# First pair's queries made inside the projection's last block, and the v blocks put ahead of the c blocks

## The chip, the core and the metric

The kernel runs on one core of a Trainium2 chip. The metric is the device time of one execution in microseconds (us). The engines are named as in the profile: PE (TensorE matmul), DVE (VectorE), ACT (ScalarE), POOL (GpSimd), and SP, which here only issues DMAs.

## The reference

Two layers of a hybrid block run over 1024 latent tokens and 256 context tokens, with a model width of 1024. Each layer computes:

```
h = modulated RMSNorm of x (latent) and ctx (context)
q, k, v, z_a, b, a, q_a, kv_a, z_b, hh, bg, cg, z_c = split(h @ w_in)
A: q,k,v = silu(depthwise conv of q,k,v); gated DeltaNet over chunks of 64 rows, both directions, 4 heads of 128
B: queries = rmsnorm(q_a) @ w_qb, rotary on 32 of 96 columns; keys, values = rmsnorm(kv_a) @ w_kvb;
   softmax attention of 4 heads, times silu(z_b)
C: bg * conv3(cg * hh) * silu(z_c)
x = x + gate * (concat(A, B, C) @ w_out)
```

The context goes through the same layer in layer 0. In layer 1 it feeds only keys, values and the DeltaNet state. All is in float32.

## The kernel before

**Precision.** Every wide product is made of three fp32r products: a tensor is split into a high part (a copy by ACT, L75) and a low part (a subtraction, L76, on DVE for the weights), and high x high, high x low and low x high are summed in PSUM. In the trace `h_hi`, `h_lo` and `w` are such parts; `h_c` are those of the 256 context tokens.

**The projection.** `run_blocks(blocks, hooks)` (L766) walks over 24 blocks of 128 output columns. A block is a weight load of 512 KB (`load`), its split into a buffer pair of pool W8 (`split`), and 24 matmuls for each group of tokens (512, 512, and the context's 256; layer 1 leaves the context out for the q, z and c blocks). While block q runs on PE, block q+2 is split and block q+3 is loaded; W8 has two buffers. The list `bl` holds in this order: four k blocks; q and z_a blocks mixed, six; eight c blocks (two groups of four: pad, times gate, convolution of three taps, times gate, times silu); four v blocks; two z_b blocks. A v or k or q block is followed by a convolution of five taps (L458 to L498): its taps are `L466`, one DVE instruction each, four of them on DVE. After a v block there come transposes on PE (L516), a scaling on DVE (`L519`, tile `sg`) and a store of `sg` to the scratch `vr_d` (L530). A z_b block ends in a silu by ACT (L566, tile `zs`) and a store to `zb_d` (L568). `sg`, `zs`, the padded rows and the accumulators share pool T5, which has five buffers.

**Beside it.** `hooks` start other work at given blocks: the preparation of the DeltaNet chunks, the inverse of their 32-row bases (L669 to L685, a chain of 31 steps of `L680` and `L681` on DVE in each of three batches), the merges of the inverses into `N` and `nn_d` (L700 to L760), and at block 21 the lanes `kv_lane`. A lane loads 128 token rows of the key and value part (`mk`, L824), transposes them on PE (L827, L828) and copies the parts into `ckv` (128 rows) and `pes` (rotary rows).

**The queries.** `load_qkv` runs behind the split of the last block but one: it loads the query and key weights, scales and splits them into `wq` (pool W8) and `wk`, and starts `q_rows`, which loads the query rows (`mq`) and a rotary table (`rot`), transposes them (L854, L855) and splits them into `qa` and `qb`. `q_head` makes one head's queries: five matmuls (L84, `qa,wq` and `qb,wq`), then an ACT copy, two rotary products on DVE (L883, L884), their sum on POOL (L885), an ACT copy (L79, `qt<-r`), and two subtractions for the low part (L887 on POOL, L888 on DVE). `mk`, `mq`, `rot`, `qb`, `r1`, `r2` and `wk_r` share pool P2, which has seven buffers.

**The attention's opening.** From L1280 on PE's instructions stand in written order; the other engines' order is made by a scheduler in all of the program. The opening calls `key_rope` (the rotary rows `pes` are copied by DMA into `kh`, `kl` and, for the context, `kc`; L1060), then `q_head` for the first pair of heads, then `k_pair` (the pair's keys: L84, `ckv,wk`), then the scores of the attention (L1104, transposed, `kh,qt` and `kc,qt`) are mixed with the DeltaNet scan, whose operands come by DMA into `ring` tiles from `vr_d`, `nn_d`, `kt_d` and `qk_d` (L1203, L1206). The first scan product is L1238. All DMAs of the program are issued by SP, in order, on one queue.

Of the kernel before, what the change touches and what calls it, by code (L numbers as in the profile page):

```python
# [8 lines left out]
F32R = mybir.dt.float32r  # L9
ACTF = mybir.ActivationFunctionType  # L10
ALU = mybir.AluOpType
# [17 lines left out]
def kernel(  # L29
# [27 lines left out]
    def st(shape, tag, dtype=F32, name=None):  # L57
        return sb.tile(shape, dtype, tag=tag, name=name or tag, bufs=BUFS[tag])
# [10 lines left out]
    V, A, P, T, S = nc.vector, nc.scalar, nc.gpsimd, nc.tensor, nc.sync  # L69
# [4 lines left out]
    def split(raw, hi, lo, eng=V):  # L74
        A.activation(out=hi, in_=raw, func=ACTF.Copy)  # L75
        eng.tensor_tensor(out=lo, in0=raw, in1=hi.bitcast(F32), op=ALU.subtract)  # L76

    def copy_a(out, in_):
        A.activation(out=out, in_=in_, func=ACTF.Copy)  # L79
# [41 lines left out]
    sch = Sched()  # L121
# [194 lines left out]
    for l in range(DEPTH):  # L316
        last = l == DEPTH - 1
        n_act = NX if last else NT
        col = LY[l]["col"]
# [113 lines left out]
        def parts(n_tok):  # L433
            return [(g, t0, n, 2 + t0 if g < 2 else 1030) for g, (t0, n) in enumerate(GROUPS) if t0 < n_tok]
# [331 lines left out]
        def run_blocks(blocks, hooks):  # L766
            n = len(blocks)
            for q in range(n):
                if q in hooks:
                    hooks[q]()  # L770
                b = blocks[q]
                for n_g, (g, _, w, _) in enumerate(parts(b.n_tok)):
                    b.mm(g)
                    if n_g == 0 and q > 1 and blocks[q - 2].post1:
                        blocks[q - 2].post1(blocks[q - 2])
                if q + 2 < n:
                    blocks[q + 2].split()
                if q + 3 < n:
                    blocks[q + 3].load()
                if q == n - 2:  # L780
                    load_qkv()
                b.post0(b)


        qkv = {}
        sc = 96.0 ** -0.5

        def load_qkv():
            wq_r = st([128, 2, 4, 128], "P4", name="wq_r")
            hq = mla_w_qb[l].rearrange("p (h f) -> p h f", h=4)  # L790
            S.dma_start(out=wq_r[:, 0, :, 0:96], in_=hq[0:128])
            for r in range(2):
                S.dma_start(out=wq_r[64 * r:64 * r + 64, 1, :, 0:96], in_=hq[128:192])
            wk_r = st([128, 512], "P2", name="wk_r")
            for w in range(2):
                S.dma_start(out=wk_r[:, 256 * w:256 * w + 256].rearrange("p (h f) -> p h f", h=4),
                            in_=mla_w_kvb[l].rearrange("p (h s f) -> s p h f", h=4, s=2)[w])
            wq = st([128, 4, 4, 128], "W8", F32R, name="wq")
            for b_ in range(2):
                V.tensor_scalar(wq_r[:, b_, :, 0:96], wq_r[:, b_, :, 0:96], col[:, 75 + b_:76 + b_], sc, ALU.mult, ALU.mult)  # L800
                P.tensor_scalar(wq_r[:, b_, :, 96:128:2], wq_r[:, b_, :, 65:96:2], -1.0, None, ALU.mult)
                P.tensor_copy(out=wq_r[:, b_, :, 97:128:2], in_=wq_r[:, b_, :, 64:96:2])
            split(wq_r[:, 0], wq[:, 0], wq[:, 1])
            copy_a(wq[:, 2], wq_r[:, 1])
            V.tensor_tensor(out=wq[0:64, 3], in0=wq_r[0:64, 1], in1=wq[0:64, 2].bitcast(F32), op=ALU.subtract)
            P.memset(wq[64:128, 3].bitcast(F32), 0.0)
            wk = st([128, 2, 512], "P4", F32R, name="wk")
            V.tensor_scalar(wk_r, wk_r, col[:, 77:78], None, ALU.mult)
            split(wk_r, wk[:, 0], wk[:, 1])
            qkv.update(wq=wq, wk=wk)  # L810
            sch.add(q_rows(qgs[0]))

        kvf = Flags()

# [22 lines left out]
        qgs = [g for g in (0, 1, 2) if g < 2 or not last]  # L837
        QA, Q = {}, {}
# [54 lines left out]
        bl = [conv_block("k", h) for h in range(4)]  # L893
        bl += [conv_block("q", 0), z_block(O_ZA, 2, za_d), conv_block("q", 1), z_block(O_ZA, 3, za_d)]
        bl += [conv_block("q", h) for h in range(2, 4)]
        bl += [c_block(j, q) for j in range(2) for q in range(4)]
        bl += [conv_block("v", h) for h in range(4)]
        bl += [z_block(O_ZB, j, zb_d) for j in range(2)]
        todo = [0, 1, 2, 3, 8, 9, 4, 5, 6, 7] if last else list(range(NT))

# [21 lines left out]
        if l == 0:  # L922
# [16 lines left out]
            for t in (0, 1):  # L939
                for hf in range(2):  # L940
                    pms = [bank(), bank()]
                    for k4 in range(2):
                        for j in range(2):
                            q = 2 * hf + j
# [91 lines left out]
        if last:  # L1036
            sch.add(adas())
        run_blocks(bl, {4: start_prep, 5: start_base, 11: start_prep_q, 8: start_merge, 21: start_kv})
        sch.until(lambda: len(kvf) == NT)
        wk, ckv, pes = qkv["wk"], qkv["c"], qkv["pe"]  # L1040
# [151 lines left out]
        units = []  # L1192
# [91 lines left out]
        def heads(u):  # L1284
            return [(u["g"], 2 * u["pair"] + r) for r in range(2)]

        key_rope()
        sch.until(lambda: qgs[0] in QA)
        for gh in heads(units[0]):
            q_head(*gh)  # L1290
        for _ in k_pair(0):
            pass
        sch.tick(3.0)
# [257 lines left out]
```

## Time and profile before

| | us |
|---|---|
| median of 3 runs (1711.97, 1713.01, 3195.78) | 1713.01 |
| the profiled execution | 1712.38 |
| its span, first to last instruction | 1710.7 |
| PE busy (96% of the span) | 1648.7 |
| DVE busy (64%) | 1095.8 |
| ACT busy (44%) | 760.1 |
| POOL busy (37%) | 632.7 |

The mean granted clock of TensorE is 0.984 of full speed. An engine's busy time is the time in which at least one of its instructions ran. In the rows below, `x8` behind a tile's name is a count of instructions, and a square bracket gives the idle time of the engine just before the instruction and what ended it. The projection of layer 0 ends on PE at 545 us, that of layer 1 at 1366 us; the opening of the attention follows each.

### The profile page before, as it was taken

How to read it: one execution, taken by the hardware profiler on the slowest of the kernel's cores; microseconds unless marked ns; L12 is line 12 of the kernel's file. 1: busy time of each engine (PE TensorE's matmuls, PEld its weight loads, DVE VectorE, ACT ScalarE, POOL GpSimd, SP SyncE). 2: the span in 40 equal slices, each digit the busy share in tenths (PEclk: the TensorE clock that was granted, in tenths of full speed). 3: DMA queues.
4: the chain of work that ended last, by engine and by line, in shares of the span. 5: the costliest groups of instructions: out<-in, count | busy, mean ns of one | idle time of the engine just before them, and what ended most of it. 6: DMA issues, size and time to landing. Idle time of an engine off the chain costs nothing.

```text
span 1710.7 us, 29900 instructions
## 1 busy us (share of the span) xinstructions
PE 1648.7 (96%) x10964; PEld 1311.5 (77%) x10964; DVE 1095.8 (64%) x2041; ACT 760.1 (44%) x1909; POOL 632.7 (37%) x848
## 2 busy tenths in 40 slices
PE   7999999999998999998999999999999979999998
PEld 5887888787887877765788887777777768776586
DVE  2534648888355767765566345589996577766664
ACT  4744554422444543344354435544335444434432
POOL 0420334332221456557331211544222135557731
PEclk9999999999999899999999999999999989999999
DMA  9332466464145745544442313564543464555541
GB/s 359 129 127 79 156 210 226 126 206 163 59 133 144 253 160 180 184 145 148 145 142 98 120 56 114 180 206 159 191 133 110 128 214 163 161 185 161 175 157 49
DMA packets 195402, 266.54 MB, mean 156 GB/s; under 512 B 50528, under 2 KB 115248, under 8 KB 195256
## 3 DMA queue, kind: packets, MB, share of 16 engines
q1 hardware_dynamic: 195256, 264.64, 47.5%
q8 instruction: 87, 1.43, 0.3%
q14 instruction: 59, 0.48, 0.1%
HBM read 182.71 MB, written 79.17 MB: 153 GB/s over the span
## 4 chain that ended last, share of the span: by engine, by line
PE 71%; DVE 10%; DMA 7%; issue 4%; ACT 3%; POOL 3%; SPq 1%; DVEq 0%; POOLq 0%; ACTq 0%
PE bank L452 27%; PE bank L84 23%; PE bank L1161 4%; PE bank L1238 2%; PE bank L1257 2%; PE bank L1104 2%; PE bank L1251 2%; PE bank L1256 2%; DVE pr L680 2%; PE bank L1228 2%; DVE Mb L681 1%; PE bank L516 1%; DVE acc L466 1%; POOL gcb L617 1%; DMA wa<-in_w_ada_dram 1%
## 5 line engine op out<-in xcount | busy, mean ns | idle before, releaser
L452 PE MATMUL bank<-h_hi,w 128*128 128x512 f32 x1664 | 432.4, 402 | 2.4 <-DVE h_hi L283 2.4
L452 PEld LDWEIGHTS bank<-h_hi,w 128*128 128x128 f32 x1664 | 303.6, 188 | 74.6 <-issue 4.5
L452 PE MATMUL bank<-h_lo,w 128*128 128x512 f32 x832 | 216.5, 401 | 0.0
L452 PEld LDWEIGHTS bank<-h_lo,w 128*128 128x128 f32 x832 | 153.3, 188 | 37.3 <-issue 2.1
L466 DVE SCALAR_TENSOR_TENSOR acc<-pad,col,acc 128x1284 f32<-128x1284 f32 (+1 forms) x104 | 157.4, 1513 | 10.5 <-ACT acc L463 8.3
L1131 POOL TENSOR_TENSOR vt<-vt,probT 128x512 f32<-128x512 f32 x110 | 143.7, 1324 | 19.0 <-ACT probT L1145 18.1
L84 PE MATMUL bank<-wo_hi,mix 128*128 128x512 f32 x576 | 146.7, 405 | 1.6 <-ACT wo_hi L75 1.3
L1145 ACT ACTIVATE probT<-bank 128x512 f32<-128x512 f32 (+1 forms) x168 | 96.5, 590 | 98.7 <-PE bank L84 92.3
L84 PEld LDWEIGHTS bank<-wo_hi,mix 128*128 128x128 f32 x576 | 109.3, 192 | 29.0 <-ACT wo_hi L75 2.8
L76 DVE TENSOR_TENSOR w<-wr,w 128x1024 fp32r<-128x1024 f32 x52 | 65.4, 1260 | 97.5 <-ACT w L75 97.4
L1106 DVE TENSOR_REDUCE mx<-bank 128x1 f32<-128x512 f32 (+1 forms) x200 | 108.5, 584 | 10.1 <-PE bank L1104 8.9
L452 PE MATMUL bank<-h_c,w 128*128 128x256 f32 x816 | 109.1, 286 | 0.0
L452 PEld LDWEIGHTS bank<-h_c,w 128*128 128x128 f32 x816 | 101.5, 188 | 6.1 <-issue 4.1
L75 ACT ACTIVATE w<-wr 128x1024 fp32r<-128x1024 f32 x52 | 55.0, 1061 | 85.0 <-PE bank L452 66.1
L84 PE MATMUL bank<-qt,kh 97*128 97x512 f32 (+1 forms) x256 | 84.5, 411 | 3.6 <-ACT probT L1145 3.3
L1161 PE MATMUL bank<-probT,vt 128*64 128x512 f32 (+1 forms) x336 | 81.1, 605 | 0.0
L1234 POOL TENSOR_TENSOR ring<-ring,qx 128x512 f32<-128x512 f32 x32 | 41.5, 1298 | 93.4 <-DMA ring<-row_d 71.2
L681 DVE TENSOR_TENSOR Mb<-Mb,pr 128x31 f32<-128x31 f32 (+15 forms) x186 | 70.4, 379 | 5.0
L84 PE MATMUL bank<-wo_lo,mix 128*128 128x512 f32 x288 | 73.5, 395 | 0.0
L680 DVE TENSOR_TENSOR pr<-L,Mb 128x31 f32<-128x31 f32 (+15 forms) x186 | 69.7, 375 | 4.8
L617 POOL TENSOR_TENSOR gcb<-gcb,gc 128x1024 f32<-128x1024 f32 x20 | 43.6, 2184 | 67.4 <-DMA gcb<-row_d 43.0
L522 ACT ACTIVATE jk<-bank 128x128 f32<-128x128 f32 x152 | 42.1, 277 | 51.5 <-PE bank L516 29.2
(309 smaller groups left out, 3201.4 us busy)
## 6 DMA issues: line engine op xcount, KB each, us to landing
wr<-in_w_blk_dram SPq DMA_DIRECT2D x52, 512.0 KB
wa<-in_w_ada_dram SPq DMA_DIRECT2D x32, 512.0 KB
gcb<-row_d SPq DMA_DIRECT2D x20, 512.0 KB
nn_d<-N SPq DMA_DIRECT2D x20, 512.0 KB
ring<-vr_d SPq DMA_DIRECT2D x40, 256.0 KB
ring<-nn_d SPq DMA_DIRECT2D x40, 256.0 KB
qk_d<-gcb SPq DMA_DIRECT2D x18, 512.0 KB
ring<-kt_d SPq DMA_DIRECT2D x36, 256.0 KB
```

Source lines behind the costliest of these rows:

```text
L75: A.activation(out=hi, in_=raw, func=ACTF.Copy)
L76: eng.tensor_tensor(out=lo, in0=raw, in1=hi.bitcast(F32), op=ALU.subtract)
L84: T.matmul(outp, lhsT=lh, rhs=rh, start=q == 0, stop=q == n - 1)
L452: T.matmul(pb[:, 0:n], lhsT=self.w[:, wi, k, :], rhs=hg[g][hi][:, k, :], start=q + k == 0, stop=q == 2 and k == KD - 1)
L466: V.scalar_tensor_tensor(out=acc[:, 2:hi], in0=pad[:, 2 + t - r:hi + t - r], scalar=col[:, ci:ci + 1], in1=acc[:, 2:hi], op0=ALU.mult, op1 ...
L617: P.tensor_tensor(gcb, gcb, bc(gc[:, i, :], 128), ALU.subtract)
L680: V.tensor_tensor(out=pv, in0=bc(L[:, 0:k, k], w), in1=N[:, k:k + 1, k:32].to_broadcast([128, k, w]), op=ALU.mult)
L681: V.tensor_tensor(out=N[:, 0:k, k:32], in0=N[:, 0:k, k:32], in1=pv, op=ALU.subtract)
L1106: V.tensor_reduce(mx[:, gk:gk + 1], pb[:, 0:n], AX.X, ALU.max)
L1131: P.tensor_tensor(acc, a0, a1, ALU.add)
L1145: A.activation(out=pts[r][:, kk, 0:n], in_=pb, func=ACTF.Exp)
L1161: T.matmul(u["po"][64 * r:64 * r + 64, 0:n], lhsT=vx[:, kt, hh * 64:hh * 64 + 64], rhs=pts[r][:, kk, 0:n], start=kt == keys[0], stop=kt == ...
```

## The change

The list of blocks has the four v blocks ahead of the eight c blocks. `load_qkv` is cut in two: loads, scaling and the split of the key weights run one block earlier (at `n - 3`), and the new `split_qkv`, at the old place, splits the query weights and starts `first_queries`, which is `q_rows` followed by `q_head` for the first pair's two heads. The opening of the attention no longer calls `q_head`; it waits, in the building of the program, for both heads to have been placed. Lines from the middle on stand 12 further down (L1104 is L1116, L824 is L836, L885 is L897, L1060 is L1072).

```diff
--- before.py
+++ after.py
@@ -777,8 +777,10 @@
                     blocks[q + 2].split()
                 if q + 3 < n:
                     blocks[q + 3].load()
+                if q == n - 3:
+                    load_qkv()
                 if q == n - 2:
-                    load_qkv()
+                    split_qkv()
                 b.post0(b)
 
 
@@ -795,20 +797,30 @@
             for w in range(2):
                 S.dma_start(out=wk_r[:, 256 * w:256 * w + 256].rearrange("p (h f) -> p h f", h=4),
                             in_=mla_w_kvb[l].rearrange("p (h s f) -> s p h f", h=4, s=2)[w])
-            wq = st([128, 4, 4, 128], "W8", F32R, name="wq")
             for b_ in range(2):
                 V.tensor_scalar(wq_r[:, b_, :, 0:96], wq_r[:, b_, :, 0:96], col[:, 75 + b_:76 + b_], sc, ALU.mult, ALU.mult)
                 P.tensor_scalar(wq_r[:, b_, :, 96:128:2], wq_r[:, b_, :, 65:96:2], -1.0, None, ALU.mult)
                 P.tensor_copy(out=wq_r[:, b_, :, 97:128:2], in_=wq_r[:, b_, :, 64:96:2])
+            wk = st([128, 2, 512], "P4", F32R, name="wk")
+            V.tensor_scalar(wk_r, wk_r, col[:, 77:78], None, ALU.mult)
+            split(wk_r, wk[:, 0], wk[:, 1])
+            qkv.update(wq_r=wq_r, wk=wk)
+
+        def first_queries():
+            yield from q_rows(qgs[0])
+            for h in range(2):
+                yield 1.2
+                q_head(qgs[0], h)
+
+        def split_qkv():
+            wq_r = qkv["wq_r"]
+            wq = st([128, 4, 4, 128], "W8", F32R, name="wq")
             split(wq_r[:, 0], wq[:, 0], wq[:, 1])
             copy_a(wq[:, 2], wq_r[:, 1])
             V.tensor_tensor(out=wq[0:64, 3], in0=wq_r[0:64, 1], in1=wq[0:64, 2].bitcast(F32), op=ALU.subtract)
             P.memset(wq[64:128, 3].bitcast(F32), 0.0)
-            wk = st([128, 2, 512], "P4", F32R, name="wk")
-            V.tensor_scalar(wk_r, wk_r, col[:, 77:78], None, ALU.mult)
-            split(wk_r, wk[:, 0], wk[:, 1])
-            qkv.update(wq=wq, wk=wk)
-            sch.add(q_rows(qgs[0]))
+            qkv["wq"] = wq
+            sch.add(first_queries())
 
         kvf = Flags()
 
@@ -893,8 +905,8 @@
         bl = [conv_block("k", h) for h in range(4)]
         bl += [conv_block("q", 0), z_block(O_ZA, 2, za_d), conv_block("q", 1), z_block(O_ZA, 3, za_d)]
         bl += [conv_block("q", h) for h in range(2, 4)]
+        bl += [conv_block("v", h) for h in range(4)]
         bl += [c_block(j, q) for j in range(2) for q in range(4)]
-        bl += [conv_block("v", h) for h in range(4)]
         bl += [z_block(O_ZB, j, zb_d) for j in range(2)]
         todo = [0, 1, 2, 3, 8, 9, 4, 5, 6, 7] if last else list(range(NT))
 
@@ -1285,9 +1297,7 @@
             return [(u["g"], 2 * u["pair"] + r) for r in range(2)]
 
         key_rope()
-        sch.until(lambda: qgs[0] in QA)
-        for gh in heads(units[0]):
-            q_head(*gh)
+        sch.until(lambda: (qgs[0], 1) in Q)
         for _ in k_pair(0):
             pass
         sch.tick(3.0)
```

The first place is SP's queue at the end of layer 0's projection. `mk` are the key rows of the last lanes, `kh`, `kl` and `kc` take the rotary rows, `ring` are the scan's operands, `zb_d` is the store of the last z_b block. Before:

```order
L824 DMA mk<-mla_d 128x160 x4
L530 DMA vr_d<-sg 128x10x128
L1060 DMA kh<-pes 33x2x1024
L1060 DMA kl<-pes 32x2x1024
L1060 DMA kh<-pes 33x2x1024
L1060 DMA kl<-pes 32x2x1024
L1203 DMA ring_5671<-vr_d 128x512
L1203 DMA ring_5671<-nn_d 128x512
L1060 DMA kc<-pes 33x2x256
L568 DMA zb_d<-zs 128x1280
L1060 DMA kc<-pes 32x2x256
```

And now:

```order
L836 DMA mk<-mla_d 128x160 x3
L1072 DMA kh<-pes 33x2x1024 x2
L1072 DMA kl<-pes 32x2x1024
L836 DMA mk<-mla_d 128x160
L1072 DMA kl<-pes 32x2x1024
L1215 DMA ring_5703<-vr_d 128x512
L1215 DMA ring_5703<-nn_d 128x512
L1215 DMA ring_5703<-kt_d 128x512
L1218 DMA ring_5703<-qk_d 128x512
L568 DMA zb_d<-zs 128x1280
L1072 DMA kc<-pes 33x2x256
```

The store `vr_d` has gone from this place, the last lane's `mk` stands behind three copies out of `pes`, and the first `kc` stands behind two more `ring` loads and the `zb_d` store.

The second place is the same stretch of SP's queue in layer 1. Before:

```order
L568 DMA zb_d<-zs 128x1024
L760 DMA nn_d<-N 128x1024
L824 DMA mk<-mla_d 128x160 x4
L530 DMA vr_d<-sg 128x10x128
L824 DMA mk<-mla_d 128x160 x2
L568 DMA zb_d<-zs 128x1024
L1060 DMA kh<-pes 33x2x1024
```

And now:

```order
L568 DMA zb_d<-zs 128x1024
L760 DMA nn_d<-N 128x1024
L836 DMA mk<-mla_d 128x160 x3
L568 DMA zb_d<-zs 128x1024
L836 DMA mk<-mla_d 128x160 x4
L1072 DMA kh<-pes 33x2x1024 x2
L1072 DMA kl<-pes 32x2x1024
```

The `mk` loads of the last four lanes now stand behind the store of the last z_b block instead of ahead of it. Of these four loads the built program lets the first wait for POOL's L897 of the first head and the third for POOL's L899 of that head, whose tiles `r2` and `r1` had their buffers of P2, and the fourth for the transposes of the first.

The third place is DVE in layer 0's projection, among the steps of the base inverse; here a piece of the difference, with - for before and + for now:

```order
 L681 TENSOR_TENSOR Mb<-Mb,pr 128x28x4
 L680 TENSOR_TENSOR pr<-L,Mb 128x135
+L466 SCALAR_TENSOR_TENSOR acc<-pad,col_103,acc 128x1284
 L681 TENSOR_TENSOR Mb<-Mb,pr 128x27x5
+L466 SCALAR_TENSOR_TENSOR acc<-pad,col_103,acc 128x1284
 L680 TENSOR_TENSOR pr<-L,Mb 128x156
+L708 STREAM_TRANSPOSE tt<-tt 128x256
+L216 TENSOR_TENSOR A_105<-bank,col_107 128x2x2
+L466 SCALAR_TENSOR_TENSOR acc<-pad,col_103,acc 128x1284
 L681 TENSOR_TENSOR Mb<-Mb,pr 128x26x6
```

The taps of the v blocks' convolutions now stand between the steps of the inverse, where the c blocks' products stood.

On PE, the ten matmuls of the first pair's queries stand in layer 0 ahead of the last block's 24 context matmuls (`h_c,w`), where they stood behind them, and in layer 1 among the last block's eight last `h_hi,w` matmuls. In layer 1 the transposes of the last seven lanes stand behind that block, where four lanes' stood.

## Rows read from the trace of the kernel before

**Rows 1.** Page, chain that ended last: shares of the span by engine.

```profile
PE 71%; DVE 10%; DMA 7%; issue 4%; ACT 3%; POOL 3%; SPq 1%; DVEq 0%; POOLq 0%; ACTq 0%
```

**Rows 2.** Windows, both projections: length, busy us PE, PEld, DVE, ACT, POOL, clock, DMA share, GB/s.

```profile
300.00:420.00 120.00, 118.56 (x1040) 95.51 (x1040) 102.79 (x214) 36.33 (x104) 37.34 (x51) 1.00 0.49 158
420.00:540.00 120.00, 120.00 (x1236) 97.52 (x1235) 58.04 (x83) 52.64 (x120) 24.16 (x53) 1.00 0.35 110
1160.00:1280.00 120.00, 120.00 (x1040) 95.97 (x1039) 111.07 (x232) 42.71 (x117) 42.27 (x67) 1.00 0.53 171
1280.00:1360.00 80.00, 79.50 (x931) 63.78 (x931) 47.45 (x62) 42.39 (x94) 16.94 (x39) 1.00 0.37 117
```

**Rows 3.** Timeline, SP, layer 0: start, duration, queue and line, [idle before <- releaser].

```profile
546.90 1.27 SPq L1203 DMA_DIRECT2D ring<-nn_d  x1
548.28 0.88 SPq L1060 DMA_DIRECT2D kc<-pes  x1
549.21 0.50 SPq L568 DMA_DIRECT2D zb_d<-zs  x1
549.81 3.24 SPq L1060 DMA_DIRECT2D kc<-pes  x3
```

**Rows 4.** Timeline, PE, layer 0, opening of the attention.

```profile
545.11 0.87 PE L84 MATMUL bank<-qa,wq 128*128 128x512 f32 x3
...
547.46 1.91 PE L84 MATMUL bank<-ckv,wk 128*128 128x512 f32 x9
...
550.65 0.50 PE L1104 MATMUL bank<-kh,qt 96*128 96x512 f32 x1 [1.29 <-ACT qt L79]
...
554.99 0.55 PE L1104 MATMUL bank<-kc,qt 96*128 96x256 f32 x1 [3.26 <-DMA kc<-pes]
```

**Rows 5.** Chain in order of time, layer 0: start, duration, what.

```profile
548.28 6.57 DMA kc<-pes
```

**Rows 6.** Windows, layer 0, two microseconds at the wait for `kc`.

```profile
552.00:554.00 2.00, 0.00 (x0) 0.00 (x0) 2.00 (x5) 1.92 (x4) 1.93 (x3) 0.75 0.89 324
```

**Rows 7.** Timeline, PE, layer 1, opening of the attention.

```profile
1366.93 0.30 PE L827 MATMUL bank<-cst,mk 128*128 128x128 f32 x1 [0.77 <-DMA mk<-mla_d]
...
1367.31 0.94 PE L84 MATMUL bank<-qa,wq 128*128 128x512 f32 x3
...
1374.19 0.51 PE L1104 MATMUL bank<-kh,qt 96*128 96x512 f32 x1 [2.58 <-ACT qt L79]
...
1377.37 0.79 PE L1104 MATMUL bank<-kh,qt 96*128 96x512 f32 x1 [1.97 <-ACT qt L79]
...
1383.43 2.05 PE L1238 MATMUL bank<-ring 128*128 128x128 f32 x8 [1.25 <-DMA ring<-nn_d]
...
1402.56 0.27 PE L1115 MATMUL bank<-cst,nm 128*8 128x128 f32 x1 [2.17 <-DVE nm L1109]
```

**Rows 8.** Timeline, SP, layer 1.

```profile
1363.45 1.55 SPq L824 DMA_DIRECT2D mk<-mla_d  x2
...
1368.81 0.94 SPq L1060 DMA_DIRECT2D kh<-pes  x1
...
1376.06 0.67 SPq L1203 DMA_DIRECT2D ring<-vr_d  x1
```

**Rows 9.** Chain in order of time, layer 1.

```profile
1362.68 3.84 DMA vr_d<-sg
...
1366.61 1.09 ACT zs L566 x2
```

**Rows 10.** Lines 466 and 519: ns min/median/max, first and last start, forms.

```profile
L466 DVE SCALAR_TENSOR_TENSOR acc<-pad,col,acc x104: 1164/1555/1925, 138.2 to 1343.8; 128x1284 f32<-128x1284 f32 x84, 128x1024 f32<-128x1024 f32 x20
...
L519 DVE TENSOR_TENSOR sg<-bank,rki x24: 411/680/693, 480.5 to 1362.2; 128x512 f32<-128x512 f32 x16, 128x256 f32<-128x256 f32 x8
```

**Rows 11.** Lines 884 and 885, the queries' rotary products and their sum.

```profile
L884 DVE TENSOR_TENSOR r<-bank,rot x16: 695/696/697, 547.8 to 1525.0; 32x512 f32<-32x512 f32 x16
...
L885 POOL TENSOR_TENSOR r<-r,r x16: 1255/1266/1280, 548.7 to 1525.8; 32x512 f32<-32x512 f32 x16
```

## The prediction

> **What bounds the kernel now.** I read the chain that ended last first: 71% of the span is PE, 10% DVE and 7% DMA [rows 1]. So a change pays where PE stands idle, or costs where it makes PE wait. Then I read windows of the two projections. PE is full there, and the resource with least room is DVE: from 300 to 420 us it is busy for 102.79 of 120 us and from 1160 to 1280 us for 111.07 of 120, while the stretches behind them leave it half free (58.04 of 120, 47.45 of 80) [rows 2]. PE was still busy for 118.56 and 120.00 us in the tight stretches, so what DVE owes is covered by the lead of the weight splits, about one block.
>
> Last come the two openings of the attention, in PE's timeline. In layer 0 the query matmuls start at 545.11 us, `k_pair` at 547.46, and then PE waits twice: 1.29 us for `qt` from ACT and 3.26 us for `kc` from a DMA [rows 4]. The DMA wait is the harder of the two: the chain runs from the first `kc` issue through 6.57 us of transfer [rows 5], and that issue follows right behind the ring loads [rows 3]. In layer 1 PE waits 2.58 us and 1.97 us, both for `qt`, then 1.25 us for a ring load, and later 2.17 us for DVE [rows 7]. These waits are the whole stake: 1.29 + 2.58 + 1.97 = 5.84 us is what the queries' chain visibly costs.
>
> **Part 1, the queries inside the last block.** The ten matmuls are moved, not removed: from 545.11 to 547.46 us they took 2.35 us [rows 4], and they take as much inside the block, so PE's busy time is unchanged. What leaves the opening is the chain behind them: ACT copy, two DVE products of 0.695 us, a POOL sum of 1.266 us, ACT again [rows 11]. All of the 5.84 us goes if nothing else is late at the same instant. So I ask what is.
>
> *Layer 0.* The score that waited 1.29 us is followed by the one that waits for `kc`, so an earlier `qt` only lengthens the second wait. What counts is when `kc` lands. The last lane's `mk` now stands behind three copies out of `pes`, which wait for the lanes before; these stand among the query matmuls, which have moved ahead of the context matmuls, so I put the first copy near 543.7 us, an estimate from that place. By the issue times of such copies (0.88 us, three in 3.24 us [rows 3]) `mk` is issued some 3 us later, at 546.7, and needs about 3 us to be used (in layer 1 two loads are issued from 1363.45 for 1.55 us, and the transposes start at 1366.93 [rows 7, 8]); with its copies on ACT and DVE the context's rotary rows are there near 550.5, so the first `kc` goes at 550 to 551 instead of 548.28. With the same 6.57 us it lands 1.7 to 2.7 us later. It also stands behind `kt`, `qk` and `zb_d` now, 256 + 256 + 640 KB by their shapes. At the 324 GB/s that the queue moved in this stretch [rows 6] these are 3.6 us if they must all pass first, and nothing if they overlap. I take +2.5 us, near the end of unchanged landing, since the ring loads ahead of `kc` before [rows 3] are already in the 6.57 us; the bounds are 0 (copies no later than now) and +6.
>
> The Trainium skill, page "DMA: Bandwidth & Descriptors", section "Queues, rings and completion order", says that SP owns one ring on each engine and that descriptors are consumed in ring order there. By that rule the 3.6 us count in full, and layer 0 would cost +5 to +6 rather than +2.5; the landing of 6.57 us for 66 KB behind larger loads agrees with it, though it doesn't separate queueing from the issue of the three further copies.
>
> *Layer 1.* Before, the last two `mk` loads wait behind the store `vr_d` and go at 1363.45 [rows 8]; their transposes start at 1366.93 [rows 7]. Now the last four stand behind the second `zb_d`, which needs the silu of the last block. The query matmuls lengthen that block by some 2.4 us, three lanes' transposes leave it (about 0.7 us), so it ends near 1367.4 and its silu (1.09 us for two [rows 9], one is left) near 1368. Then the first load's buffer must be released by POOL's sum: the first head's matmuls end near 1366, plus the ACT copy, 2 x 0.69 on DVE and 1.27 on POOL [rows 11] is about 1369. The third load waits for one more ACT copy and POOL subtraction, 1371; the fourth for the transposes of the first, 1369 + 2.9 + 0.3 = 1372.2, and lands near 1375.5. The first rotary copy `kh` then goes at about 1376 instead of 1368.81; eight such copies took until 1376.06, when the ring loads begin [rows 8]. So the ring loads start up to 6.6 us later, and the scan product at 1383.43 [rows 7], which was waiting for one, moves with them; the vanished waits of 2.58 and 1.97 are swallowed on the way. Something comes back: 4 x 0.69 us of the queries' DVE work is out of the opening, which shortens the DVE wait of 2.17 us at 1402.56. Also, the store `vr_d` with its 3.84 us, for which the last silu waited [rows 9], is gone from this place, so the block's end may come earlier than I have it. I take +5 us; the bounds are -4.5 (both `qt` waits gone, nothing later) and +8.
>
> **Part 2, v ahead of c.** Neither the work nor PE's count of matmuls changes; DVE's is shifted. A v block costs four taps of 1.555 us and a scaling of 0.68 + 0.68 + 0.41 (1.77): 8.0 us, four of them 32 us. A group of four c blocks costs two taps and three products of the shape of that scaling: 3.1 + 5.3 = 8.4 us [rows 10]. So the tight stretch, in which one such group stood, gets about 23 us more of DVE work in each layer. Its free DVE time was 120 - 102.79 = 17.2 us in layer 0 and 8.9 us in layer 1 [rows 2]; 6 to 14 us overflow into the freer stretch behind. The cover is the lead of the splits, about one block (a block with three groups takes near 15 us of PE, one with two groups near 12). I put the stalls at +1 us in all, from 0 to +4 while the cover holds; if it is gone the overflow itself is the price, 6 + 14 = 20 us. The loads and scaling that `load_qkv` does one block earlier lie in a stretch where DVE and POOL are half idle, as the second and fourth of the rows show [rows 2]: 0. The two stores `cx_d` that now take the place of `vr_d` near the end have no reader at the opening: 0.
>
> **The sum.** +2.5 + 5 + 1 = +8.5 us on the profiled execution's 1712.4, so 1721 us. The median of the runs, 1713.0, is 0.6 us above the profiled one, which I leave out.
>
> **Rivals.**
>
> *The waits simply go* (chance 0.22). If the lanes' loads are not late, the seams lose 1.29 + 2.58 + 1.97 = 5.8 us, and up to 8 with the DVE wait of 2.17 [rows 7]: 1704 to 1707. For it speaks that `vr_d` leaves the queue in front of the lanes' loads; against it the loads' new place behind `zb_d` and the POOL releases.
>
> *It cancels* (chance 0.22). Layer 0 stays bound by `kc` as it was, layer 1 loses its `qt` waits and gains as much for `ring`: 1709 to 1716.
>
> *DVE becomes the bound of the projection: slower* (chance 0.12). In the tight stretch a weight split is queued behind a v block's four taps and the inverse's steps, and PE waits for `w`. It decides when the overflow exceeds the lead of about 12 to 15 us; layer 1's 14 us is right at it. The price is up to 20 us, with the seams as forecast 1712.4 + 20 + 7.5 = 1740. Against it: the trace shows PE full with DVE at 93% [rows 2], and inverse steps may yield to splits.
>
> In a sentence of its own: the Trainium skill, "GPSIMD Engine Reference", states that VectorE and GpSimd share their SBUF interfaces, which would make those DVE operations longer than their medians; `L466`, with a median of 1555 ns, reaches 1925 [rows 10], which would agree, and it would only raise the price of this rival.
>
> The forecast has 0.44. My range goes from the best of the first rival, 1704, to 1736, which takes in the upper bounds of both seams (1712.4 + 6 + 8 + 4 = 1730) and part of the DVE case.
>
> **Chances by size.** 2% (34 us) is about what a measurement of this kernel tells from no change: faster means under 1679, slower over 1747. No case reaches the first, and only the worst of the DVE case the second: 0.02, 0.94, 0.04.
>
> **What would show it.** In the changed profile, layer 0: `kc` issued after 550 us relative to a projection that ends at 545, and PE's wait before the first `kc` score over 4 us. Layer 1: no `qt` wait, but a gap before `k_pair` or the first score that ends on `mk`, `pes` or `kh`, `mk` loads issued singly behind `zb_d`, and ring loads some 6 us later against the end of the last block. Projections: PE busy 118 to 120 in each 120 us; a gap before `L452` that ends on DVE `w` would favour the DVE case. If the lanes' last transposes lie within 2 us of the last block's end, my layer 1 term is wrong and the first rival holds.

## The result

The changed kernel takes 1729.13 us (median of six runs, 1720.80 to 1733.78), the kernel before 1711.95 us. The ratio is 1.0101, with a 95% interval from 1.0083 to 1.0119: about 17 us slower, a change of less than 2%. One of the six runs before took 3195.78 us, the others 1707.54 to 1713.01. The profiled execution is the fastest of the six, 1720.8 us with a span of 1719.0, so the trace below shows half of the loss (8.3 us of span); a second trace of the same kernel, taken in the experiments, shows more of it.

To see where the time went I set marks in both traces: a first and the last projection matmul of each layer (L452; the count begins in layer 0 with the first matmul of the context's tokens, `h_c,w`, at 104 us, and in layer 1 with its first projection matmul, near 930 us), and the first update of the scan's state behind the opening (`bank<-vd,ring`). All in us:

| | layer 0 projection | from its end to the first state update | layer 1 projection | from its end to the first state update | span |
|---|---|---|---|---|---|
| before | 440.9 | 19.3 | 435.0 | 23.6 | 1710.7 |
| changed | 444.1 | 16.2 | 444.7 | 24.8 | 1719.0 |
| changed, second trace | 446.4 | 16.7 | 449.8 | 26.3 | 1733.9 |

The ten query matmuls, 2.35 us, have moved from the openings into the projections, and the transposes of one lane in layer 0 and of three in layer 1 (0.22 us each) the other way, so +2.1 and +1.7 us of the projections are no loss. Layer 0 as a whole comes out even in the first trace (+3.2 and -3.1). Layer 1's projection is where the time is: +9.7 us in the first trace and +14.8 of the second trace's +23.2. In it PE stands idle for 8.3 us before, for 13.5 us in the first trace and 18.4 in the second. The four windows of [rows 2], in the profile of the changed kernel:

```profile
300.00:420.00 120.00, 116.17 (x1036) 95.00 (x1035) 108.58 (x190) 46.38 (x112) 39.12 (x60) 1.00 0.54 167
420.00:540.00 120.00, 120.00 (x1234) 97.06 (x1233) 49.41 (x106) 43.53 (x112) 21.54 (x44) 1.00 0.33 105
1160.00:1280.00 120.00, 114.64 (x968) 94.39 (x967) 115.28 (x203) 46.20 (x108) 41.07 (x66) 0.99 0.53 166
1280.00:1360.00 80.00, 79.35 (x939) 60.51 (x939) 40.21 (x85) 33.12 (x85) 17.80 (x38) 1.00 0.37 113
```

PE was busy for 118.56 and 120.00 us of the tight stretches; now it is for 116.17 and 114.64. DVE has gone from 102.79 to 108.58 and from 111.07 to 115.28, and it has become lighter behind them. PE's timeline shows the longest new waits there, two in each layer:

```profile
353.66 0.45 PE L720 MATMUL bank<-tt,Mm 32*32 32x32 f32 x32 [1.68 <-DVE tt L709]
...
385.14 0.45 PE L720 MATMUL bank<-tt,Mm 32*32 32x32 f32 x32 [2.15 <-DVE tt L709]
...
1203.87 3.39 PE L452 MATMUL bank<-h_hi,w 128*128 128x512 f32 x8 [2.50 <-DVE tt L738]
...
1232.27 0.23 PE L729 MATMUL bank<-tt 32*32 32x32 f32 x4 [1.91 <-ACT tt L723]
```

None of them waits for a weight. L720 and L729 are steps of the merges, which stand at fixed places in PE's order; L720 needs a scaling on DVE (L709), L729 a copy by ACT (L723). The third wait is that of a projection matmul that the profile puts behind L738, a merge's scaling that reads from a PSUM bank. The eight matmuls behind the third wait took 3.39 us (why is told at the end).

The openings, in the order of [rows 3], [rows 4], [rows 7] and [rows 8]. Layer 0, SP and then PE:

```profile
547.37 1.57 SPq L836 DMA_DIRECT2D mk<-mla_d  x1
...
552.06 0.37 SPq L568 DMA_DIRECT2D zb_d<-zs  x1
...
554.20 3.21 SPq L1072 DMA_DIRECT2D kc<-pes  x4
```

```profile
552.91 0.45 PE L839 MATMUL bank<-cst,mk 128*128 128x128 f32 x1 [4.44 <-DMA mk<-mla_d]
...
553.23 3.55 PE L84 MATMUL bank<-ckv,wk 128*128 128x512 f32 x9
...
558.60 0.35 PE L1116 MATMUL bank<-kc,qt 96*128 96x256 f32 x1 [0.33 <-DMA kc<-pes]
...
560.44 2.21 PE L1250 MATMUL bank<-ring 128*128 128x128 f32 x16
```

The last lane's `mk` went at 547.37 and the first `kc` at 554.20 instead of 548.28, behind `zb_d`. Against the end of the projection that is 5.7 us instead of 3.0; the forecast, 550 to 551 with an end at 545.3, was 4.7 to 5.7. PE waits 4.44 us for `mk` where it waited 1.29 for `qt`, but the 3.26 us for `kc` have shrunk to 0.33, and 16 scan products run without the 0.85 us wait for DVE that split them before. All waits of PE from the projection's end to the first state update add up to 5.0 us against 5.4. Layer 1, SP and PE:

```profile
1375.05 0.32 SPq L568 DMA_DIRECT2D zb_d<-zs  x1
...
1375.78 3.54 SPq L836 DMA_DIRECT2D mk<-mla_d  x4
...
1380.17 1.87 SPq L1072 DMA_DIRECT2D kh<-pes  x2
...
1387.42 0.59 SPq L1215 DMA_DIRECT2D ring<-vr_d  x1
```

```profile
1378.30 0.45 PE L839 MATMUL bank<-cst,mk 128*128 128x128 f32 x1 [3.03 <-DMA mk<-mla_d]
...
1381.23 3.34 PE L84 MATMUL bank<-ckv,wk 128*128 128x512 f32 x9
...
1388.39 0.55 PE L1116 MATMUL bank<-kc,qt 96*128 96x256 f32 x1 [3.00 <-DMA kc<-pes]
...
1391.93 4.15 PE L1250 MATMUL bank<-ring 128*128 128x128 f32 x16 [1.28 <-DMA ring<-nn_d]
```

The four `mk` stand behind the store at 1375.05, take 3.54 us to issue, the rotary copies start 6.0 us after the end of the projection (3.1 before), and the ring loads 13.3 us after it (10.3 before). The waits for `qt` are gone; waits for `mk`, `kc` and a ring load have their place, 8.3 us in all against 7.3. Behind the waits for `mk` the granted clock is 0.50 (from 552 to 558 us and from 1378 to 1384 us), and `k_pair`'s nine matmuls take 3.55 and 3.34 us instead of 1.91 and 1.90.

### The profile page after: what moved, and what is told of

Same layout as the page of the kernel before. It is cut to its first block, busy times and chain, and to the rows that moved or that the text cites. A ratio compares the mean times of both kernels' runs of the same rounds, so it can differ in the third digit from the quotient of the medians.

```text
span 1719.0 us, 29914 instructions
## 1 busy us (share of the span) xinstructions
PE 1646.0 (96%) x10964; PEld 1309.0 (76%) x10964; DVE 1095.4 (64%) x2041; ACT 759.3 (44%) x1909; POOL 632.7 (37%) x848
## 4 chain that ended last, share of the span: by engine, by line
PE 74%; DVE 9%; DMA 6%; issue 4%; POOL 3%; ACT 3%; SPq 1%; POOLq 0%; DVEq 0%; ACTq 0%
PE bank L452 30%; PE bank L84 22%; PE bank L1173 3%; PE bank L1250 2%; PE bank L1269 2%; PE bank L1263 2%; PE bank L1268 2%; PE bank L1116 2%; PE bank L1240 2%; DVE acc L466 1%; DVE Mb L681 1%; PE bank L188 1%; DVE pr L680 1%; DMA wa<-in_w_ada_dram 1%; PE bank L516 1%
## 5 line engine op out<-in xcount | busy, mean ns | idle before, releaser
L452 PE MATMUL bank<-h_hi,w 128*128 128x512 f32 x1664 | 434.9, 403 | 4.9 <-DVE tt L738 2.5
L452 PEld LDWEIGHTS bank<-h_hi,w 128*128 128x128 f32 x1664 | 305.1, 189 | 77.9 <-issue 7.2
L452 PE MATMUL bank<-h_lo,w 128*128 128x512 f32 x832 | 215.7, 400 | 0.0
L452 PEld LDWEIGHTS bank<-h_lo,w 128*128 128x128 f32 x832 | 153.4, 188 | 37.4 <-issue 2.1
L452 PE MATMUL bank<-h_c,w 128*128 128x256 f32 x816 | 108.2, 286 | 0.1
L452 PEld LDWEIGHTS bank<-h_c,w 128*128 128x128 f32 x816 | 101.6, 189 | 6.2 <-issue 4.1
L84 PEld LDWEIGHTS bank<-wo_lo,mix 128*128 128x128 f32 x288 | 54.1, 188 | 13.1
```

Of the source, the lines that this page charges most:

```text
L84: T.matmul(outp, lhsT=lh, rhs=rh, start=q == 0, stop=q == n - 1)
L452: T.matmul(pb[:, 0:n], lhsT=self.w[:, wi, k, :], rhs=hg[g][hi][:, k, :], start=q + k == 0, stop=q == 2 and k == KD - 1)
```

## The experiments

The marks of all of them, one traced execution each (the ratios are of several runs, each against the kernel before run beside it):

| | ratio to before, 95% interval | layer 0 projection | opening | layer 1 projection | opening |
|---|---|---|---|---|---|
| before | 1 | 440.9 | 19.3 | 435.0 | 23.6 |
| order alone | 1.0097 (1.0078 to 1.0115) | 444.5 | 16.0 | 448.3 | 24.4 |
| queries alone | 1.0030 (1.0010 to 1.0050) | 442.3 | 17.1 | 437.8 | 22.3 |
| changed, again | 1.0120 (1.0101 to 1.0139) | 446.4 | 16.7 | 449.8 | 26.3 |
| two taps left out | 1.0052 (1.0033 to 1.0071) | 440.3 | 16.5 | 443.7 | 25.7 |
| v between the c groups | 1.0145 (1.0127 to 1.0163) | 450.1 | 16.1 | 452.8 | 22.9 |
| paired key rows | 1.0119 (1.0099 to 1.0140) | 445.3 | 16.6 | 449.6 | 27.2 |
| queries alone, paired | 1.0024 (1.0010 to 1.0038) | 443.5 | 19.2 | 437.7 | 19.7 |
| before, paired | 1.0013 (1.0003 to 1.0024) | 441.1 | 18.0 | 433.6 | 22.6 |
| before, DVE load | 1.0258 (1.0241 to 1.0275) | 452.6 | 17.2 | 461.5 | 22.1 |
| before, half DVE load | 1.0093 (1.0076 to 1.0110) | 438.6 | 18.8 | 454.4 | 22.2 |
| sg apart | 1.0223 (1.0207 to 1.0239) | 442.1 | 17.4 | 444.4 | 29.2 |
| small pool cut | 1.0294 (1.0278 to 1.0310) | 445.5 | 19.1 | 453.8 | 29.7 |

### Each part alone

The kernel before with the new order only:

```diff
         bl += [conv_block("q", h) for h in range(2, 4)]
+        bl += [conv_block("v", h) for h in range(4)]
         bl += [c_block(j, q) for j in range(2) for q in range(4)]
-        bl += [conv_block("v", h) for h in range(4)]
```

> Only the order of the blocks is changed (v ahead of c); the queries stand in the opening of the attention as before. Two-cause theory (the DVE overflow in the projections and the late key rows at the openings each cost about half): PE idles 2 to 4 us more in layer 0's tight stretch and 4 to 6 us more in layer 1's, in merges that wait for DVE (tt), and the openings cost 0 to 3 us, since only the last lane's load stands behind the last store: 6 to 10 us slower than before. Rival 'the queries alone do it': within 2 us of before, with PE as full in the projections as before. Rival 'the order alone does it': as slow as the changed kernel, 9 to 17 us.

Measured: 1.0097, +14.7 us of median (1726.33 against 1711.63). The two-cause theory had half of it; the rival that gives the order 9 to 17 us holds on size. The loss is in layer 1's projection (+13.3 us in the trace), where PE is idle for 17.5 us instead of 8.3. The longest new wait is in a merge:

```profile
1274.93 0.88 PE L755 MATMUL bank<-N,tt 64*64 64x64 f32 x16 [4.43 <-ACT tt L749]
```

The changed kernel with the c blocks ahead of the v blocks again:

```diff
-        bl += [conv_block("v", h) for h in range(4)]
         bl += [c_block(j, q) for j in range(2) for q in range(4)]
+        bl += [conv_block("v", h) for h in range(4)]
```

> Only the queries are moved into the last block; the c blocks stay ahead of the v blocks. Two-cause theory: the projections are as full as before; in the openings the last lanes' loads are held back by POOL's sums of the queries, so the rotary copies and the ring loads come 3 to 6 us later in layer 1 and 0 to 2 us in layer 0: 3 to 7 us slower than before. Rival 'the order alone does it': -4 to +1 us against before, the waits for qt gone. Rival 'the queries alone do it': 9 to 17 us slower.

Measured: 1.0030, +4.9 us, the size that the two-cause theory gave. The projections are as full as before once the moved matmuls are taken off (442.3 and 437.8). The theory's mechanism is not in the trace: in layer 1 the rotary copies start 2.7 us and the ring loads 10.2 us after the projection (3.1 and 10.3 before), and the projections and openings of both layers together take 0.7 us more, of 4.6 us that the span grew; the rest lies between the layers (1.8) and behind the last opening (2.2). So what the queries' move costs, and where, stays open. Order and queries alone add up to 19.6 us; the changed kernel beside them was 19.2 us slower. So the order carries three quarters of the loss, and the queries one quarter.

### The spread of the changed kernel

> The changed kernel itself, unaltered, for its spread and a second trace: its runs lay between 1721 and 1734 us. If the spread is in the tight stretches (DVE theory), a slower execution than the first traced one shows more PE idle time there, with the openings alike; if it is in the openings (DMA theory), the later landings of mk and kc show it.

Measured: 1.0120. The traced execution spans 1733.9 us, and against the first trace 5.1 of the 14.9 us lie in layer 1's projection, all but 0.2 of them PE idle time, 2.2 in layer 0's projection, and 2.0 in the two openings. That is what the DVE theory asked for, but it is half: another 5.5 us lie between the layers and behind the last opening, which neither theory covers. New among PE's waits there:

```profile
1210.49 3.58 PE L452 MATMUL bank<-h_hi,w 128*128 128x512 f32 x8 [2.87 <-DVE tt L738]
...
1220.71 1.12 PE L755 MATMUL bank<-N,tt 64*64 64x64 f32 x16 [2.09 <-POOL pad L458]
```

`pad` is the padded row of a v block, a tile of the five-buffer pool. That brought the second suspect in: not only DVE's time, but the pool T5.

### Less DVE work in the v blocks

```diff
-                acc = conv(pad, [t * 12 + base for t in range(5)], hi)
+                acc = conv(pad, [t * 12 + base for t in range(5)] if nm != "v" else [t * 12 + base for t in range(1, 4)], hi)
```

> The changed kernel with two of the five taps of the v blocks' convolution left out, so its output is not the reference's: 16 DVE instructions of 1.55 us, some 25 us of DVE work, are gone from the tight stretches of both layers. If the DVE overflow stalls PE there (two-cause theory), 4 to 8 us come back against the changed kernel, and PE is full again from 300 to 420 and 1160 to 1280 us; the openings stay as they are. Rival (queries alone): within 2 us of the changed kernel, since DVE is not what PE waits for.

Measured: 1.0052; the median is 9.5 us under that of the changed kernel beside it (1721.23 against 1730.78), more than expected, and layer 0's projection is back at 440.3. DVE work, or the time that it keeps the tiles, is a cause. In layer 1 it is not gone: the projection takes 443.7 us there against 435.0 before, and 444.7 and 449.8 in the changed kernel's two traces, and PE is busy for 116.77 us from 1160 to 1280, not full as expected.

### The v blocks between the two c groups

```diff
-        bl += [conv_block("v", h) for h in range(4)]
-        bl += [c_block(j, q) for j in range(2) for q in range(4)]
+        bl += [c_block(0, q) for q in range(4)]
+        bl += [conv_block("v", h) for h in range(4)]
+        bl += [c_block(1, q) for q in range(4)]
```

> The changed kernel with the four v blocks between the two groups of c blocks, so that the first c group keeps its old place in the tight stretch and the v blocks come where DVE is half free. DVE-overflow theory: the projections are as full as with the queries' move alone (layer 1's first to last projection matmul 285 to 288 us against 292.6 in the changed kernel), and the whole is 1712 to 1719 us. Rival (what costs is any move of v, by its stores and buffers): it stays within 4 us of the changed kernel, 1725 or more.

The 285 to 288 and 292.6 us in this expectation count from a matmul 152 us later; in the table's count they are 437 to 440 and 444.7.

Measured: 1.0145, the slowest order of all, 6.7 us above the changed kernel, beyond the rival's 4 us as well; layer 1's projection takes 452.8 us. My DVE-overflow theory, in the form that the first place alone is tight, falls. PE's timeline shows one long wait in layer 1, and the chain of waits (start, duration, what) what stood behind it:

```profile
1291.73 0.65 PE L720 MATMUL bank<-tt,Mm 32*32 32x32 f32 x32 [9.52 <-DVE tt L709]
```

```profile
1272.86 1.62 DVE sg L519 x3
...
1274.51 4.15 DMA vr_d<-sg
...
1278.76 1.38 ACT acc L463
...
1280.17 1.56 DVE acc L466
...
1287.67 0.32 POOL tt L706
...
1288.10 2.11 DMA tt<-blk_o
...
1291.05 0.55 DVE tt L709
```

Read from the top: a v block's `sg` is scaled, its store to `vr_d` takes 4.15 us, only then has ACT a buffer for the next accumulator, DVE adds its taps in between the steps of the inverse, and only then POOL gets the merge's tile `tt` (L706), whose load and scaling PE is waiting for. The buffers are handed on in a row; the v blocks put a store of 640 KB into it.

### DVE's time by itself

The kernel before, with reductions added on DVE. They use no tile of the pools but the one they read; the other instructions stay the same in number, though some change places, since the scheduler orders all anew:

```diff
             def post0(b):
                 pr = parts(n_tok_a)
+                if j == 0:
+                    for _ in range(6 if part < 3 else 4):
+                        V.tensor_reduce(dum[:, 0:1], KQ["q"][0][:, 3, :], AX.X, ALU.max)
```

> The kernel before, with 22 reductions over 1024 columns added on DVE in each layer while the first group of c blocks runs: about 1.07 us each, 23 us a layer, the surplus that the v blocks would bring to that place, but with no tile of the five-buffer pool, no store and no other engine. If DVE's time is what the new order costs, PE's merges wait for DVE (tt) in the tight stretches and the run is 8 to 14 us slower than before. Rival (the v blocks' tiles: pads, accumulators and sg hold the five buffers until the vr_d store lands, and the merges' tiles wait for them): within 2 us of before.

Measured: 1.0258, over three times the upper end of what was expected. Each reduction took 1.21 us, 26.5 us a layer. Layer 0's projection grew by 11.7 us and layer 1's by 26.5, and in each nearly all of it shows as one wait of PE, in layer 0 for a small ACT copy and in layer 1 in a merge (lines from the middle on stand 4 further down: L724 is L720):

```profile
358.22 1.02 PE L210 MATMUL bank<-cst,ms 128*128 128x2 f32 x4 [11.05 <-ACT ms L79]
...
1230.13 0.65 PE L724 MATMUL bank<-tt,Mm 32*32 32x32 f32 x32 [23.38 <-DVE tt L713]
```

Then half the load, `range(3 if part < 3 else 2)`:

> The kernel before with 11 instead of 22 added reductions a layer: 1.2 us each as measured with 22, 13 us a layer. The tight stretches of before left 17.2 us of DVE free in layer 0 and 8.9 us in layer 1. Threshold theory (DVE's free time covers what is added until it is used up): nothing in layer 0, 0 to 6 us in layer 1, the whole 0 to +6 us. Rival (cost in proportion to the load, since the merges' chain on DVE is delayed from the first microsecond on): half of the 43 us of the full load, +15 to +25 us.

Measured: 1.0093, +16.1 us, in the range of the proportion and not of the threshold theory. But the marks separate the layers. From the first projection matmul to the first state update layer 0 took 460.3 us before, 457.4 with the half load and 469.8 with the full one: there the free DVE time of 17.2 us covers 13 us and not 26.5, as the threshold theory said. In layer 1 that theory falls: 13 us of load make one wait of 13.0 us, 26.5 make one of 23.4. The chain of waits that ends it, with the half load:

```profile
1203.27 0.58 DVE L L688
...
1203.86 1.04 DVE L L689
...
1204.92 2.60 DMA blk_o<-L
...
1207.95 2.21 DMA tt<-blk_o
...
1210.18 0.45 DVE tt L712
...
1210.88 0.55 DVE tt L713
...
1211.47 0.54 PE bank L724 x23
```

The base inverse ends on DVE (L688 and L689, before L684 and L685), its blocks go out and come back by DMA (2.60 and 2.21 us), DVE transposes and scales them (L712, L713), and PE goes on. This chain of layer 1 has no slack against the place where the merge stands on PE. That 8.9 of 120 us were free in the window says nothing about it.

These runs do not price the new order. A load of 26.5 us a layer cost 43 us, while the order, with some 23 us a layer more, cost 14.7. In the traces the merges' places on PE are not the same: the second merge of layer 1 stands behind 912 of the layer's projection matmuls in the kernel before and with both loads, and behind 984 with the new order. So with the new order more projection work stands ahead of that merge. That this is why the order costs less than its load alone is argued here, not tested.

### The five buffers

`sg` in a buffer of its own, with the small pool cut from seven to five for the room; and the control, the small pool cut alone:

```diff
-    BUFS = {"B16": 7, "B4": 2, "W8": 2, "T5": 5, "P4": 4, "P2": 7, "sm": 4, "h5": 2, "br": 1, "st": 8}
+    BUFS = {"B16": 7, "B4": 2, "W8": 2, "T5": 5, "P4": 4, "P2": 5, "sm": 4, "h5": 2, "br": 1, "st": 8, "sg": 1}
...
-                    sg = st([128, NT, 128], "T5", name="sg")
+                    sg = st([128, NT, 128], "sg", name="sg")
```

> The changed kernel with sg in a buffer of its own, so that no v block's store holds one of the five buffers; the small pool has five buffers instead of seven to make room. Buffer rival: against the run with the small pool alone cut, 5 to 10 us come back, and the waits for vr_d of the pads, accumulators and merge tiles are gone. DVE theory: within 3 us of that run.

> The changed kernel with the small pool cut from seven buffers to five and nothing else, the control for the run with sg apart. Late-key-rows theory: fewer buffers hold the last lanes' rows back further, so the openings grow and it is 2 to 10 us slower than the changed kernel; rival (the small pool does not matter): within 2 us of it.

Measured: 1.0294 for the cut alone, 1.0223 with `sg` apart: 12.0 us come back (1758.30 to 1746.32), more than the 5 to 10 expected. The intervals lie apart. The projections explain it: 3.4 us in layer 0 and 9.4 in layer 1. In the changed kernel the waits of layer 0's tight stretch (us in total, times, longest) name the store, and they are gone with `sg` apart, as are those of layer 1:

```profile
POOL pad L458 <- DMA vr_d<-sg: 9.4, 2, 9.0
...
POOL tt L706 <- DMA vr_d<-sg: 5.5, 1, 5.5
```

So the buffer rival holds as well, beside DVE's time; whether it is the store, or only that five buffers are too few once `sg` is among them, this run does not separate. How much of the order's 14.7 us belongs to each I can't say: both act through the same merges, and the runs were made on different bases. The control itself lost more than expected, 1.0294 against the changed kernel's 1.0120: its trace is 26.1 us longer than the changed kernel's second one, of which 3.4 lie in layer 1's opening and 16.7 behind it, so most of that is not in the openings, where the key rows are. It was not followed further.

### Key rows in pairs

`kv_lane` loads two lanes' rows by one DMA:

```diff
-            mk = st([128, 160], "P2", name="mk")
-            S.dma_start(out=mk, in_=mla_d[i, :, 0:160])
+            mk2 = st([128, 2, 160], "P2", name="mk")
+            S.dma_start(out=mk2, in_=mla_d[i:i + 2, :, 0:160].rearrange("i p f -> p i f"))
...
-            sch.pool([kv_lane(i) for i in range(NT)], 3)
+            sch.pool([kv_lane(i) for i in range(0, NT, 2)], 3)
```

> The changed kernel with the key rows of two lanes loaded by one DMA into one buffer: five loads instead of ten, so fewer stand behind the last store and fewer buffers of the small pool are asked for. Late-key-rows theory: in layer 0 the wait of 4.4 us for mk shrinks below 3, in layer 1 the waits of 3.0 + 0.7 us for mk shrink by half, and 3 to 7 us come back against the changed kernel; the tight stretches stay as they are. Rival (kc and the ring loads bind the openings whatever the lanes do): within 2 us of the changed kernel, the waits only named otherwise.

Measured: 1.0119, the same as the changed kernel. The waits for `mk` are gone in layer 0, and the first score runs 1.6 us after the projection instead of 8.1, but the `kc` wait takes all of it:

```profile
559.26 0.55 PE L1120 MATMUL bank<-kc,qt 96*128 96x256 f32 x1 [6.32 <-DMA kc<-pes]
```

In layer 1 a wait of 1.75 us for `mk` is left, and waits of 4.12 and 1.53 us for ring loads follow. The rival holds: `kc` and the ring loads bind the opening, and the late rows had been waiting in their shadow.

> The queries' move alone (c ahead of v as before) with the paired key rows. If the late key rows are all that the queries' move costs, the waits for mk go (2.97 us in layer 0, 1.94 us in layer 1 of the queries' move alone) and the opening's time from the last projection matmul to the first state update falls from 17.1 to 14 to 16 us and from 22.3 to 18 to 20: 2 to 6 us faster than the queries' move alone, -4 to +1 us against the kernel before. Rival (ring loads bind): as slow as the queries' move alone, +3 to +6.

Measured: 1.0024, within the interval of the queries alone (1.0030). Layer 1's opening fell by 2.6 us as expected, layer 0's grew by 2.1 on `kc` and ring loads (4.52 and 2.74 us). The whole is in the rival's range.

> The kernel before with the paired key rows alone, a control: its openings waited for qt, kc and ring, hardly for mk (0.77 us once), so -2 to +1 us against before. Rival (the loads on SP's queue bind the opening there too): 3 us or more faster.

Measured: 1.0013: +1.9 us of median, just over the +1 expected, and no gain. No version here beats the kernel before.

## Why the prediction came out as it did

The direction and the range held: 1721 us was forecast, between 1704 and 1736, and 1729 came. The sum was right by luck. For the traced execution it is close to exact, +8.5 us forecast and +8.3 measured in the span, but its terms are not. With the moved matmuls counted where they were, layer 0's opening gave -1.0 us, layer 1's +2.9, the two projections +9.1 (1.1 and 8.0), and -2.8 lie between the layers and behind the last opening.

**Layer 0's opening (+2.5).** The step on `kc` held: its issue moved from 3.0 to 5.7 us behind the end of the projection. What it was worth did not. From the projection's end to the first state update 19.3 us became 16.2; without what was moved that is 1.0 us shorter, below my lower bound of 0. PE now stands 4.44 us waiting for `mk`, and `kc` comes in that shadow: PE waits 0.33 us for it, where I had named a wait of over 4 us as the sign. With the key rows in pairs the shadow is gone and the wait for `kc` is 6.32 us. My sum added up what `kc` was pushed behind as a cost of its own.

The Trainium skill's rule on ring order ("DMA: Bandwidth & Descriptors", section "Queues, rings and completion order") would, by my estimate, have added 3.6 us for the loads ahead of `kc`. Here `kc` was in use 4.4 us after its first issue, against 6.7 before with less ahead of it. So the trace bears out no such addition; by how much the loads ahead had drained when `kc` was issued no run here tells.

**Layer 1's opening (+5).** This held in its chain, and was sized too high. Without what was moved the opening grew by 24.8 - (23.6 - 1.7) = 2.9 us in the first trace, and by 4.4 in the second. The queue of causes was as forecast (store, four loads, rotary copies, ring loads), but the ring loads came 2.9 us later against the projection's end, not some 6. Neither part does it alone: counted the same way, the opening grew by 0.2 us with the order alone and by 1.1 with the queries alone. And relieving the loads gave nothing back with the whole change, because `kc` and ring come next.

**v ahead of c (+1): the step that failed.** I had the load about right (23 us more DVE work a layer by the program; 16 taps and 12 scalings against one group of c blocks) and its cover wrong. I put the cover at "the lead of the weight splits, about one block" and took +1, 0 to +4. In neither trace of the changed kernel is one of PE's longer waits for a split `w`, and PE was busy for 116.17 and 114.64 us of the tight stretches, not for 118 to 120. PE waits in the merges, whose place in its order is fixed and whose input comes from the end of the base inverse on DVE. In layer 0 that chain had the slack that the window's free time suggested, in layer 1 none: 13 us of load there, on the kernel before, cost a 13.0 us wait. The part was worth 14.7 us, not 1. And I had not looked at the pool T5 at all, in which a v block's `sg` waits for a store of 640 KB while the next pad, accumulator and merge tile wait for it.

**The rivals.** "DVE becomes the bound" was the nearest in size for its part (20 us, chance 0.12), with the wrong place ("PE waits for `w`") and a wrong point of decision (a lead of 12 to 15 us). "The waits simply go" did not happen: the `qt` waits went, others came. "It cancels" (1709 to 1716, chance 0.22) is about what the openings did, and the queries alone, at 1716.5; the order's 14.7 us went past it.

## What to carry to other kernels

A busy share of 85 or 93% does not tell how much work still fits: ask which chain on that engine ends in an instruction with a fixed place on the bounding engine, and measure that chain's slack, by adding work of known length to the kernel before; then look whether the change itself moves that place. When blocks trade places, compare the buffers that they hold and until which store, not only their engine time. And a wait that is taken away at an opening is worth only its distance to the next operand that is late, here `kc` and the ring loads behind `qt` and `mk`.

## What was not expected of the hardware

A wait of PE cost more than its length. With the half DVE load layer 1's projection grew by 19.4 us, of which 14.7 are more idle time of PE; the other 4.7 are longer work. The windows of two microseconds around the end of the 13.0 us wait (length, busy us of PE, PEld, DVE, ACT and POOL, granted clock, DMA share, GB/s), and eight matmuls of one kind ahead of it and behind it:

```profile
1198.00:1200.00 2.00, 0.48 (x3) 0.05 (x1) 1.84 (x4) 0.00 (x0) 0.15 (x1) 1.00 0.01 4
1204.00:1206.00 2.00, 0.00 (x0) 0.00 (x0) 1.83 (x6) 0.00 (x0) 0.31 (x1) 0.50 0.22 86
1212.00:1214.00 2.00, 2.00 (x18) 1.78 (x8) 1.86 (x5) 1.02 (x4) 0.14 (x1) 0.50 0.03 8
1216.00:1218.00 2.00, 2.00 (x7) 1.57 (x7) 1.85 (x6) 0.00 (x0) 0.00 (x0) 0.71 0.52 211
1218.00:1220.00 2.00, 2.00 (x10) 1.59 (x10) 1.85 (x5) 0.00 (x0) 0.00 (x0) 1.00 0.22 70
```

```profile
1196.46 2.03 PE L453 MATMUL bank<-h_hi,w 128*128 128x512 f32 x8
...
1214.75 3.23 PE L453 MATMUL bank<-h_hi,w 128*128 128x512 f32 x8
```

PE stopped at 1198.5. From 1204 on the granted clock was 0.50, the level of 1.2 GHz, and it was back at 1.00 only at 1218, after PE had worked from 1211.5 on: the eight matmuls took 3.23 us instead of 2.03. The short wait of 2.50 us in the changed kernel had the same effect, 0.50 from 1204 to 1206 us. But not every short wait had: behind those of 1.91 and 2.15 us the clock stayed at 1.00.

```profile
1204.00:1206.00 2.00, 2.00 (x5) 1.61 (x6) 1.97 (x5) 1.36 (x2) 0.00 (x0) 0.50 0.03 8
...
1234.00:1236.00 2.00, 2.00 (x12) 1.64 (x11) 1.82 (x7) 1.37 (x2) 0.00 (x0) 1.00 0.03 8
...
386.00:388.00 2.00, 2.00 (x19) 2.00 (x18) 1.97 (x4) 1.18 (x4) 0.00 (x0) 1.00 0.91 252
```

So a short wait, of which the changed order makes several, can cost speed behind it. Which ones do is not told by their length alone: the one of 2.15 us was not followed by a lower clock, but one of 2.09 us in the second trace, at 1220.71, was:

```profile
1222.00:1224.00 2.00, 2.00 (x10) 2.00 (x11) 0.07 (x1) 1.99 (x3) 0.00 (x0) 0.50 0.02 4
```
